# 1/|k| by Newton's method on GpSimd, in place of a square root on ScalarE, in a streaming encoder step

## The chip, the cores and the metric

The kernel runs on one core of a Trainium2 chip. The metric is the device time of one execution in microseconds (us); the figure for a kernel is the median of several runs. A core has five engines, each with a queue of its own that it works off in order: TensorE (PE; its weight loads are shown apart as PEld), VectorE (DVE), ScalarE (ACT), GpSimd (POOL) and SyncE (SP, which here issues the DMAs). The engines wait for each other by semaphores.

## The reference

One layer of an encoder on 1024 prompt frames and 32 frames of a running stream. One input projection feeds four branches; each is projected again, gated and summed; an output projection and a layer norm end it. The change lies in branch D, the gated delta rule, which works on eight heads of width 128:

```
def l2norm(x):
    return x * lax.rsqrt(jnp.sum(x * x, axis=-1, keepdims=True) + L2_EPS)
...
q = l2norm(qkv[..., :W_QK].reshape(bsz, l, H_D, DK))
k = l2norm(qkv[..., W_QK:2 * W_QK].reshape(bsz, l, H_D, DK))
beta = jax.nn.sigmoid(col(OFF_DB, H_D).astype(f32))
...
kb = k * beta[..., None]
a_mat = jnp.where(strict, jnp.einsum('nbhid,nbhjd->nbhij', kb, k) * decay, 0.0)
t_mat = a_mat + jnp.eye(c, dtype=a_mat.dtype)
u_base = lax.linalg.triangular_solve(t_mat, v * beta[..., None], left_side=True,
                                     lower=True, unit_diagonal=True)
```

So each frame of each head needs 1/|k|: one number per frame, from the sum of 128 squares.

## The kernel before

The 1056 frames lie along the free dimension, in chunks of 352 columns. A list of jobs runs on PE: each loads 128 columns of a weight matrix (512 KB, `wr`), splits it into a high part on ScalarE (`wh`, L179) and a low part on VectorE (`wl`, L181), and multiplies it with the normalised input, split likewise (`xh`, `xl`, L212), into PSUM tiles named `mm`, which ScalarE or VectorE evict. Weights are loaded one job ahead.

Beside the jobs run queues of background steps, written as Python generators. At fixed points of each job (`bg()`) every queue is advanced by its rate, so its instructions are recorded between the job's. The framework then orders the instructions of each engine and sets the semaphores; engines execute in that order. Two kinds of background step matter here:

- Convolutions (`conv`, L312, L315 and L318): ScalarE starts an accumulator, then VectorE adds one tap after another over about 1060 columns, 1.3 us each. There are short ones (4 taps, `acc`) and one of 31 taps per channel block (`accc`).
- `gdn_a(h)`, the first stage of the delta rule for head h, between about 100 and 460 us. Its PSUM tiles are named `aux`; there are four such banks, used in turn.

In `gdn_a` the frames of a head lie in nine groups of 128 (the ninth has the 32 frames of the running stream). For groups 0 to 3, 4 to 7 and 8 in turn, PE transposes k and q (L478), ScalarE squares each group with a sum along the row (L480, into `kss` and `qss`), and VectorE forms `ke` from the transposed k (L483), which frees the bank. Then come four numbers per frame, for all nine groups at once (tiles of 128x9): r2 = 1/(kss + eps), cb = beta r2, c2 = -cb e^g, and c1 = beta sqrt(r2), for which ScalarE takes the square root (L492). After that, for each set of groups: PE transposes v (L527) and VectorE multiplies it by c1 (R, L529), which frees the bank of the transposed v, and R is stored to memory (`d_r<-st`); PE multiplies k with k and q (L546, two groups of six matmuls); VectorE scales and masks the result (L537 with cb, L538 with EU), which frees those banks. The tiles `st` that hold R, A and PT have two buffers each in turn, so that L538 of a set waits for the store of R. ScalarE makes the decays by Abs and Exp (L505, L506, L508), GpSimd masks them (EU, L507), and VectorE scales q (L509). GpSimd also fills and copies the few history columns of each convolution (`pad`, L292 and L296; `st_d`, L304 and L305).

On ScalarE each of these functions needs a table: ACT_TABLE_LOAD stands ahead of an instruction whose function is not in the loaded one. Silu (L428), Sigmoid (L748), Exp and Sqrt alternate in this stretch.

## Time and profile before

| | |
|---|---|
| time, three runs | 2212.17, 2213.03 (median), 2217.18 us |
| profiled execution | 2218.46 us, of which the span from first to last instruction is 2216.8 |
| busy in the span | PE 2175.4, DVE 1652.8, ACT 998.4, POOL 187.3 us |
| granted TensorE clock, mean | 0.997 |
| ACT table loads, L492 | 8, of 1283 ns each |

The profiled execution is one run, by the hardware profiler. In rows of a timeline the columns are start and duration in us, engine, line, operation, out<-in with shapes, and count; a bracket tells how long the engine was idle ahead of it and what ended that. Rows of groups show count, busy us and mean ns, then the idle time ahead. Rows of waits read: who waited, for whom, us in total, times, longest. Rows of stretches give the length and the busy us of PE, PEld, DVE, ACT and POOL (instructions in brackets), the granted clock, and DMA figures.

### The profile page before, as it was taken

The page shows a single profiled execution, that of the slowest core. Times are in us where ns is not written, and L with a number is a line of the kernel's source. Part 1 is how long each engine was busy: PE and PEld are TensorE (multiplying, and loading weights), DVE is VectorE, ACT ScalarE, POOL GpSimd, SP SyncE. Part 2 cuts the span into 40 slices and gives each one's busy share as a digit, 9 for nine tenths or more (in the row PEclk, how much of TensorE's full clock was granted, in tenths as well). Part 3 has the DMA queues.
Part 4 walks back from the last instruction along what each step waited for, and adds up shares of the span by engine and source line. Part 5 has one row for each costly group of instructions (what it writes and reads, how often), then busy time and mean ns, then how long its engine had stood idle before and what let it go on. Part 6 is the DMA issues. An engine that isn't in the chain of part 4 may idle for free.

```text
span 2216.8 us, 38575 instructions
## 1 busy us (share of the span) xinstructions
PE 2175.4 (98%) x15334; PEld 2127.1 (96%) x15334; DVE 1652.8 (75%) x2668; ACT 998.4 (45%) x1938; POOL 187.3 (8%) x257
## 2 busy tenths in 40 slices
PE   7999999999999999999999999999999999999998
PEld 7998999999999998999999999999999999999986
DVE  8585898569994764788979879767767779745576
ACT  4587668621124543333444444467677345203200
POOL 2211332001010000000000000000000000000043
PEclk9999999999999999999999999999999999999999
DMA  6144445431227764224333323333333889975422
GB/s 238 49 129 111 120 125 140 116 122 58 69 58 231 228 185 115 83 89 134 100 117 114 122 97 131 111 106 130 128 117 124 324 329 330 333 244 174 137 88 85
DMA packets 198159, 323.70 MB, mean 146 GB/s; under 512 B 52793, under 2 KB 117131, under 8 KB 197659
## 3 DMA queue, kind: packets, MB, share of 16 engines
q1 hardware_dynamic: 197979, 321.25, 45.0%
q8 instruction: 120, 1.97, 0.4%
q14 instruction: 60, 0.49, 0.1%
HBM read 211.12 MB, written 110.06 MB: 145 GB/s over the span
## 4 chain that ended last, share of the span: by engine, by line
PE 78%; DVE 3%; ACT 2%; DMA 2%; issue 1%; SPq 0%; DVEq 0%; ACTq 0%
PE mm L212 34%; PE mm L1091 28%; PE mm L1455 4%; PE mm L224 3%; PE aux L1204 1%; PE mm L240 1%; DMA wr<-in_w_in 1%; PE mm L1435 1%; PE aux L719 1%; PE aux L699 1%; PE aux L706 1%; PE aux L718 1%; PE aux L690 1%; PE aux L655 0%; PE aux L649 0%
## 5 line engine op out<-in xcount | busy, mean ns | idle before, releaser
L315 DVE SCALAR_TENSOR_TENSOR accc<-padc,cols,accc 128x1086 f32<-128x1086 f32 (+1 forms) x249 | 335.6, 1348 | 8.9 <-ACT accc L312 7.1
L212 PE MATMUL mm<-xh,wh 128*128 128x352 f32 (+2 forms) x1600 | 292.8, 324 | 1.8 <-ACT xh L898 0.9
L212 PE MATMUL mm<-xl,wh 128*128 128x352 f32 (+2 forms) x1600 | 290.7, 323 | 0.0
L212 PE MATMUL mm<-xh,wl 128*128 128x352 f32 (+2 forms) x1568 | 286.2, 323 | 0.0
L212 PEld LDWEIGHTS mm<-xh,wh 128*128 128x128 f32 x1600 | 256.3, 189 | 3.6 <-DVE xh L896 1.1
L212 PEld LDWEIGHTS mm<-xl,wh 128*128 128x128 f32 x1600 | 256.3, 189 | 1.4 <-issue 0.4
L212 PEld LDWEIGHTS mm<-xh,wl 128*128 128x128 f32 x1568 | 251.1, 189 | 1.2 <-issue 0.2
L179 ACT CAST wh<-wr 128x1024 fp32r<-128x1024 f32 x96 | 100.6, 1048 | 299.8 <-PE mm L212 226.6
L1091 PE MATMUL mm<-xh,o 128*128 128x264 f32 x1152 | 216.8, 284 | 0.0
L1091 PEld LDWEIGHTS mm<-xh,o 128*128 128x128 f32 x1152 | 181.3, 188 | 0.0
L1091 PE MATMUL mm<-xl,o 128*128 128x264 f32 x576 | 163.8, 284 | 0.0
L1103 ACT COPY mu<-mm 128x264 f32<-128x264 f32 x216 | 80.2, 376 | 158.8 <-PE mm L1091 157.9
L181 DVE TENSOR_TENSOR wl<-wr,wh 128x1024 fp32r<-128x1024 f32 x96 | 117.0, 1218 | 32.1 <-ACT wh L179 20.8
L1091 PE MATMUL mm<-xh,wl 128*128 128x264 f32 x576 | 113.7, 287 | 3.8 <-ACT mu L1103 3.8
L1091 PE MATMUL mm<-th,o 128*128 128x264 f32 x576 | 113.1, 286 | 1.5 <-ACT mu L1103 1.4
L1091 PE MATMUL mm<-xh,wh 128*128 128x264 f32 x576 | 111.8, 285 | 1.1 <-ACT xh L1154 1.1
L1091 PE MATMUL mm<-th,wh 128*128 128x264 f32 x576 | 111.6, 285 | 0.0
L1091 PE MATMUL mm<-th,wl 128*128 128x264 f32 x576 | 111.0, 285 | 0.0
L1109 DVE TENSOR_TENSOR ev<-mm,mu 128x264 f32<-128x264 f32 x216 | 91.5, 427 | 25.1 <-ACT mu L1103 12.6
L1091 PEld LDWEIGHTS mm<-xl,o 128*128 128x128 f32 x576 | 108.3, 188 | 0.0
L1287 DVE TENSOR_TENSOR ev<-mm,ev 128x352 f32<-128x352 f32 x90 | 46.0, 522 | 82.6 <-PE mm L212 71.9
L1056 DVE TENSOR_TENSOR o<-wr,o 128x512 fp32r<-128x512 f32 x108 | 74.1, 686 | 40.9 <-ACT o L1055 40.4
(341 smaller groups left out, 4954.4 us busy)
## 6 DMA issues: line engine op xcount, KB each, us to landing
wr<-in_w_in SPq DMA_DIRECT2D x137, 512.0 KB, 3.7
d_z<-ev SPq DMA_DIRECT2D x64, 264.0 KB, 2.1
d_gate<-ev SPq DMA_DIRECT2D x64, 264.0 KB, 2.1
wr<-in_w_branch SPq DMA_DIRECT2D x32, 512.0 KB, 5.5
ev<-d_gate SPq DMA_DIRECT2D x30, 528.0 KB, 7.3
st<-d_t SPq DMA_DIRECT2D x28, 528.0 KB, 6.5
sl<-d_z SPq DMA_DIRECT2D x28, 528.0 KB, 7.2
d_mix<-ev SPq DMA_DIRECT2D x24, 528.0 KB, 3.6
```

Source lines behind the costliest of these rows:

```text
L179: act.copy(hi, raw)
L181: dve.tensor_sub(lo, raw, hi.bitcast(F32))
L212: pe.matmul(ps[:, :c[1]], lhsT=w[:, k, :], rhs=r(k)[:, cs(c)], start=(n == 0), stop=(n == len(todo) - 1))
L224: pe.matmul(ps[:, :c[1]], lhsT=w[:, k, :], rhs=r(k)[:, cs(c)], start=(n == 0), stop=(n == len(todo) - 1))
L240: pe.matmul(ps[:, :c[1]], lhsT=w[:, k, :], rhs=j.rhs[r](k)[:, cs(c)], start=(k == i == 0), stop=(k == KT - 1 and i == 2))
L315: dve.scalar_tensor_tensor(acc, pad[:, i:i + W], col(name, ci, i), acc, op0=OP.mult, op1=OP.add)
L1056: dve.tensor_sub(t[:, 4:8], src, t[:, 0:4].bitcast(F32))
L1091: pe.matmul(b, lhsT=w[:, wo + k, :], rhs=XS[name](p, k)[:, sl], start=(start and n == 0), stop=(stop and n == 11), skip_group_check=True)
L1103: act.copy(mu[name][:, c * HC:(c + 1) * HC], b)
L1109: dve.tensor_add(res[i][:, a:a + HC], b, mu[name][:, c * HC:(c + 1) * HC])
L1287: dve.tensor_mul(G[d][:, cs(c)], ps, G[d][:, cs(c)])
L1455: pe.matmul(ps, lhsT=a[k][:, ts], rhs=w[k][:, hs], start=(n == 0), stop=(n == len(todo) - 1))
```

## The change

The square root on ScalarE goes. VectorE makes a first value of 1/sqrt(kss + eps) out of the bits of the number, by a shift and a subtraction in integers read as such (two instructions). GpSimd scales kss + eps by -0.5 and then runs three Newton steps r1 <- r1 (1.5 - 0.5 (kss + eps) r1^2), four instructions each. VectorE multiplies the result with beta, as before. All tiles are 128x9.

```
         r2 = gp.tile([128, 9], F32, name="r2")
-        dve.tensor_scalar(r2, kss[:, :, h], L2_EPS, None, op0=OP.add)
-        dve.reciprocal(r2, r2)
+        k2 = gp.tile([128, 9], F32, name="k2")
+        r1 = gp.tile([128, 9], F32, name="r1")
+        dve.tensor_scalar(k2, kss[:, :, h], L2_EPS, None, op0=OP.add)
+        dve.reciprocal(r2, k2)
         dve.tensor_mul(cb[:, :, h], r2, beta[:, :, h])
         dve.scalar_tensor_tensor(c2[:, :, h], cb[:, :, h], -1.0, egc[:, :, h], op0=OP.mult, op1=OP.mult)
-        act.activation(r2, r2, AF.Sqrt)
-        dve.tensor_mul(c1[:, :, h], r2, beta[:, :, h])
+
+        I32 = mybir.dt.int32
+        dve.tensor_scalar(r1.bitcast(I32), k2.bitcast(I32), 1, None, op0=OP.logical_shift_right)
+        dve.tensor_scalar(r1.bitcast(I32), r1.bitcast(I32), -1.0, float(0x5f3759df), op0=OP.mult, op1=OP.add)
+        pool.tensor_scalar(k2, k2, -0.5, None, op0=OP.mult)
+        for _ in range(3):
+            pool.tensor_tensor(r2, r1, r1, op=OP.mult)
+            pool.tensor_tensor(r2, r2, k2, op=OP.mult)
+            pool.tensor_scalar(r2, r2, 1.5, None, op0=OP.add)
+            pool.tensor_tensor(r1, r1, r2, op=OP.mult)
+        dve.tensor_mul(c1[:, :, h], r1, beta[:, :, h])
```

Lines behind the change count 11 more in the changed kernel: c1 is L504 there (L493 before), R is L540 (L529), the matmul groups are L557 (L546). The framework orders the instructions anew. Three places, all in head 0, show what this does.

VectorE, before. L493 forms c1 (here `c_130`), L529 forms R from it, and L315 are taps of a convolution:

```order
L483 TENSOR_TENSOR st<-aux,eks 32x128
L488 TENSOR_SCALAR r_1490<-kss 128x9
L489 RECIPROCAL r_1490<-r_1490 128x9
L490 TENSOR_TENSOR cb<-r_1490,beta 128x9
L491 SCALAR_TENSOR_TENSOR c_131<-cb,egc 128x9
L315 SCALAR_TENSOR_TENSOR acc<-pad,cols,acc 128x1059 x2
L493 TENSOR_TENSOR c_130<-r_1490,beta 128x9
L529 TENSOR_TENSOR st<-aux,c_130 128x512
```

VectorE, now, at the same place:

```order
L490 TENSOR_SCALAR k_1491<-kss 128x9
L491 RECIPROCAL r_1490<-k_1491 128x9
L496 TENSOR_SCALAR r_1492<-k_1491 128x9
L492 TENSOR_TENSOR cb<-r_1490,beta 128x9
L497 TENSOR_SCALAR r_1492<-r_1492 128x9
L493 SCALAR_TENSOR_TENSOR c_131<-cb,egc 128x9
L315 SCALAR_TENSOR_TENSOR acc<-pad,cols,acc 128x1059
L504 TENSOR_TENSOR c_130<-r_1492,beta 128x9
L315 SCALAR_TENSOR_TENSOR acc<-pad,cols,acc 128x1059
L540 TENSOR_TENSOR st<-aux,c_130 128x512
```

Two instructions are added, and one of the two taps that stood ahead of c1 now stands between c1 and R. In heads 1, 2, 5 no tap stands between the first value (L497) and c1; in head 3 there are two, in head 4 two, in heads 6 and 7 small instructions. In heads 6 and 7 a weight split (L181) now stands between c1 and R.

GpSimd, now. The names `r_1492` and `r_1490` are r1 and r2, `k_1491` is k2:

```order
L305 COPY st_d<-pad 128x3
L498 TENSOR_SCALAR k_1491<-k_1491 128x9
L500 TENSOR_TENSOR r_1490<-r_1492 128x9
L501 TENSOR_TENSOR r_1490<-r_1490,k_1491 128x9
L502 TENSOR_SCALAR r_1490<-r_1490 128x9
L503 TENSOR_TENSOR r_1492<-r_1492,r_1490 128x9
```

The last four rows stand there three times, and the copies of the next convolution's history (L304, L305) follow them. Before, nothing stood between these copies and those ahead. Each of these instructions waits for a semaphore that tells of the one before. In head 3 a mask of the decays (L518, L507 before) of 128x512 stands right ahead of the chain.

ScalarE, before:

```order
L480 ACTIVATE junk,qss<-aux 32x128
L312 ACTIVATE acc<-pad,cols 128x1059
L492 ACT_TABLE_LOAD
L492 ACTIVATE r_1490<-r_1490 128x9
L418 COPY pad<-mm 128x352 x2
L179 CAST wh<-wr 128x1024
```

ScalarE, now:

```order
L480 ACTIVATE junk,qss<-aux 32x128
L312 ACTIVATE acc<-pad,cols 128x1059
L418 COPY pad<-mm 128x352 x2
L179 CAST wh<-wr 128x1024
L516 ACTIVATE E<-E 32x32
L519 ACT_TABLE_LOAD
```

The load and the root are gone, and the load for the exponential (L519, L508 before) stays. In the whole program 92 table loads are left of 102. On PE the same matmuls stand in nearly the same order: in head 0 the group L557 stands one matmul earlier, in head 2 the transposes of v and the groups behind them stand 18 matmuls of the jobs later, and elsewhere no group is moved by more than seven. After the stretch of `gdn_a` the order is the same but for a few instructions on each engine.

## The prediction

> **What bounds the kernel now.** I read the page first, then the stage table of the stretch in which the changed lines run (110 to 460 us, heads 0 to 7 of the delta branch), then who waits for whom there, and last the rows around each of the eight places, in order of time.

> ```profile
> PE 2175.4 (98%) x15334; PEld 2127.1 (96%) x15334; DVE 1652.8 (75%) x2668; ACT 998.4 (45%) x1938; POOL 187.3 (8%) x257
> PE 78%; DVE 3%; ACT 2%; DMA 2%; issue 1%; SPq 0%; DVEq 0%; ACTq 0%
> ...
> 110.00:460.00 350.00, 338.40 (x2205) 330.66 (x2204) 259.35 (x478) 251.31 (x574) 64.22 (x105) 1.00 0.47 124
> 460.00:900.00 440.00, 440.00 (x3040) 423.93 (x3039) 332.37 (x573) 145.20 (x332) 31.74 (x33) 1.00 0.44 131
> ```

> TensorE (PE) is busy for 98% of the span, and the chain that ended last is PE for 78%. So the time is PE's work, plus the holes in it. Then comes the stretch of the change (busy PE, weight load, VectorE, ScalarE, GpSimd): PE is busy 338.4 of 350 us, so it has 11.6 us of holes. A change here can win at most these, and it loses what it adds to them. What ends them, and what VectorE (DVE) waits for at the changed line:

> ```profile
> PE aux L478 <- DVE st L483: 6.1, 3, 4.4
> PE aux L478 <- ACT junk L480: 2.4, 3, 1.0
> PE aux L527 <- DVE st L483: 2.0, 2, 1.8
> PE aux L546 <- DVE st L538: 0.6, 1, 0.6
> PE aux L546 <- DVE st L529: 0.3, 1, 0.3
> ...
> DVE c L493 <- ACT r L492: 11.2, 5, 3.1
> ```

> The columns are total us, times, longest. PE waits for 11.4 us in all, all of it for VectorE or ScalarE (ACT) to free one of the four "aux" PSUM banks. VectorE waits at c1 (L493) in five of eight heads, 11.2 us in all, for the square root.

> **The change part by part.**

> *ScalarE.* It loses, in each head, the table load and the square root:

> ```profile
> 132.22 1.28 ACT L492 ACT_TABLE_LOAD   x1
> 133.52 0.21 ACT L492 ACTIVATE r<-r 128x9 f32<-128x9 f32 x1
> ```

> That is 8 x 1.49 = 11.9 us. The order has 92 table loads where it had 102, so two more go by themselves: 2.6 us. ScalarE thus gets 14.5 us back, of which only what PE waits for counts: at most the 2.4 us of "L478 <- ACT junk", which I book whole as a gain, and, one step removed, part of the 8.1 us for st L483, which itself waits for ScalarE's squares. I book none of that (rival C does). [...]

> *GpSimd.* It gains 13 steps per head on 128x9, each reading what the one before wrote. The trace has no such row. The nearest:

> ```profile
> L1443 POOL TENSOR_TENSOR padc<-padc,wh 128x1024 f32<-128x1024 f32 x8 | 20.0, 2505 | 0.6
> ...
> L899 POOL TENSOR_TENSOR xl<-z,xh 128x128 fp32r<-128x128 f32 x2 | 0.9, 456 | 0.5 <-ACT xh L898 0.5
> ...
> 312.54 0.19 POOL L304 COPY st_d<-pad 128x3 f32<-128x3 f32 x1 [2.75 <-ACT pad L418]
> ```

> From 128 to 1024 columns a product grows by (2505 - 456) / 896 = 2.29 ns a column, so at 9 columns it is 456 - 119 x 2.29 = 184 ns, as the copy of three columns (0.19). L1443 reads what the instruction before it wrote, and idles 0.6 / 8 = 0.075 us for that. So I take 0.26 us a step, an estimate: 3.1 us for the 12 steps behind the first value, 3.4 for all 13. Bounds: 0.19 (no wait between steps; 2.3 us) and 0.456 (the shortest product seen; 5.5 us). A gain below these is excluded, since all steps hang on each other.

> These steps share something with VectorE:

> ```profile
> 140.11 1.28 DVE L318 SCALAR_TENSOR_TENSOR ev<-pad,cols,acc 128x1024 f32<-128x1024 f32 x1 [1.00 <-PE aux L527]
> ...
> 227.84 0.20 POOL L507 TENSOR_SCALAR_AFFINE_SELECT EU<-E 32x32 f32<-32x32 f32 x1 [20.42 <-DVE Gb L509]
> 140.49 0.97 POOL L507 TENSOR_SCALAR_AFFINE_SELECT EU<-E 32x32 f32<-32x32 f32 x1 [1.99 <-ACT E L506]
> 258.53 6.05 POOL L507 TENSOR_SCALAR_AFFINE_SELECT EU<-E 128x512 f32<-128x512 f32 x1
> ```

> The same select takes 0.20 us alone, and 0.97 when it meets the convolution step L318: it ends at 141.46, just as L318 does (141.39). One takes 6.05 us while VectorE runs such steps back to back. I read this as GpSimd standing still while a long two-input instruction runs on VectorE. [...] It speaks against this change: a convolution step placed beside the chain covers none of it. Without that rule head 0, below, would lose 1.7 us instead of 3.0.

> *VectorE.* Two more small instructions per head (0.15 to 0.18 us each, about 0.35) stand ahead of c1. And c1 now waits for GpSimd: behind it in VectorE's queue stands R = transposed v times c1 (L529), whose end frees the aux bank for PE's next group (L546) and whose store must land before the product at L538. So the question in each head is how late R becomes, and how much of that lies in slack.

> *Head 0.* VectorE, then PE:

> ```profile
> 131.08 0.15 DVE L488 TENSOR_SCALAR r<-kss 128x9 f32<-128x9 f32 x1
> ...
> 132.24 2.68 DVE L315 SCALAR_TENSOR_TENSOR acc<-pad,cols,acc 128x1059 f32<-128x1059 f32 x2 [0.33 <-ACT acc L312]
> 134.84 0.18 DVE L493 TENSOR_TENSOR c<-r,beta 128x9 f32<-128x9 f32 x1
> 135.10 0.69 DVE L529 TENSOR_TENSOR st<-aux,c 128x512 f32<-128x512 f32 x1
> ...
> 135.86 0.38 PE L546 MATMUL aux<-kqh 128*128 128x256 f32 x1
> ```

> Today two convolution steps cover the root, and PE's group starts at 135.86, the moment R ends (135.79): no slack. In the new order one convolution step stands ahead of c1 and one behind it. The first value is there at about 132.0; one step fits before 132.24; then GpSimd stands until 133.56; the other 11 x 0.26 = 2.9 us end at 136.5. With c1 and the second convolution step R starts at 138.0, not 135.1. PE's group stands one matmul earlier, so it waits in full: **3.0 us**.

> *The other heads* (DVE at c1 and R, PE where it has a group soon after):

> ```profile
> 167.72 0.18 DVE L493 TENSOR_TENSOR c<-r,beta 128x9 f32<-128x9 f32 x1 [3.14 <-ACT r L492]
> 173.27 0.28 PE L546 MATMUL aux<-kqh 128*128 128x256 f32 x1
> ...
> 219.18 0.18 DVE L493 TENSOR_TENSOR c<-r,beta 128x9 f32<-128x9 f32 x1 [0.86 <-ACT r L492]
> 223.50 0.69 DVE L529 TENSOR_TENSOR st<-aux,c 128x512 f32<-128x512 f32 x1 [4.15 <-DMA d_ke<-st]
> ...
> 262.66 0.15 DVE L493 TENSOR_TENSOR c<-r,beta 128x9 f32<-128x9 f32 x1
> 269.31 0.76 DVE L538 TENSOR_TENSOR st<-aux,EU 128x256 f32<-128x256 f32 x2 [2.22 <-DMA d_r<-st]
> 270.75 0.28 PE L546 MATMUL aux<-kqh 128*128 128x256 f32 x1
> ...
> 311.04 0.17 DVE L493 TENSOR_TENSOR c<-r,beta 128x9 f32<-128x9 f32 x1
> 317.25 0.76 DVE L538 TENSOR_TENSOR st<-aux,EU 128x256 f32<-128x256 f32 x2 [0.60 <-DMA d_r<-st]
> 318.16 0.28 PE L546 MATMUL aux<-kqh 128*128 128x256 f32 x1
> ...
> 353.01 0.18 DVE L493 TENSOR_TENSOR c<-r,beta 128x9 f32<-128x9 f32 x1 [2.77 <-ACT r L492]
> 394.95 0.18 DVE L493 TENSOR_TENSOR c<-r,beta 128x9 f32<-128x9 f32 x1 [3.08 <-ACT r L492]
> 395.22 0.69 DVE L529 TENSOR_TENSOR st<-aux,c 128x512 f32<-128x512 f32 x1
> 395.98 0.28 PE L546 MATMUL aux<-kqh 128*128 128x256 f32 x1
> ...
> 434.85 0.18 DVE L493 TENSOR_TENSOR c<-r,beta 128x9 f32<-128x9 f32 x1 [1.31 <-ACT r L492]
> 438.49 0.69 DVE L529 TENSOR_TENSOR st<-aux,c 128x512 f32<-128x512 f32 x1 [1.47 <-PE aux L527]
> ```

> - Head 1: VectorE is free from 164.58 (167.72 less 3.14). Two convolution steps now go ahead of the chain (2.6), then 0.35 and 3.2 (chain and hops): c1 at 170.7, 3.0 late. R then ends at 171.7, and PE's group comes at 173.27: 0.
> - Head 2: 218.32 + 0.35 + 3.2 = 221.9, but R waits for a DMA until 223.50 anyway: 0.
> - Head 3: c1 is due at 263.0, but the chain stands behind the select that took 6.05 us, and all of it runs only once VectorE stops: 0.3, taken for the rest of the select, and 3.4 for the chain, so c1 at 266.7, 4.0 late. L538 waits for R's store, so it moves along; the first of its two ends at about 269.7, 1.0 ahead of PE's group at 270.75. PE loses 3.0 there. The last 1.0 I let it lose too, in a longer wait for st L483 (1.8 is the longest of the L527 row above): **4.0 us**.
> - Head 4: two convolution steps between the first value and c1 leave the chain standing: 311.04 + 0.35 + 3.2 = 314.6; one step of like length stands between c1 and R as before: 3.3 late after what small gaps give. L538's first ends at 317.67, PE's group comes at 318.16: **2.8 us**.
> - Head 5: 350.24 + 0.35 + 3.2 = 353.8, 0.8 late; no group of PE's near: 0.
> - Head 6: c1 as late as today, but a weight split (1.2 us) now stands ahead of R, which comes 1.0 later; PE's group follows R's end (395.91) by 0.07: **0.9 us**.
> - Head 7: 433.54 + 0.35 + 3.2 = 437.1, the split 1.2: 438.3, and R waits for PE until 438.49: 0.

> On SP's queue, R's stores and the weight loads behind them move by as much as R; the loads run a whole job ahead, so I book nothing. GpSimd's own state copies behind the chain wait 3 us longer, and no row shows anyone in a hurry for them. After 460 us the order hardly differs, and PE is busy for all 440 us from there to 900, so what is lost stays lost.

> **Sum:** 3.0 + 4.0 + 2.8 + 0.9 - 2.4 = +8.3 us. The profiled execution took 2218.46 us, so it would be 2226.8; it lies 5.4 above the median of the runs, 2213.03. On the median: 2213.0 + 8.3 = **2221.3 us**.

> **The rivals.**

> *B, covered.* Head 0 pays, but elsewhere VectorE catches up before PE notices: it is busy 259 of 350 us in this stretch. For it speak heads 1, 2, 5 and 7; against it the two places with 1.0 and 0.5 us of slack. +3.0 + 0.9 - 2.4 = +1.5: 2214.5.

> *C, faster.* ScalarE's 14.5 us bring its squares forward, and with them st L483 and PE's waits for both: 6.1 + 2.4 + 2.0 = 10.5 go, head 0 and 6 take 3.9: -6.6, 2206.4. It decides once more than 3.9 us of these waits go. For it: the longest, 4.4 us at L478, comes in a row of table loads. Against it: these are loads for the exponential and the sigmoid, most of which stay, and no square root stands near.

> *D, dearer steps.* At 0.456 us a step the chain is 5.5 us, 2.4 more; heads 0, 3, 4 and 6 pay it in full and heads 1, 5 and 7 some 0.5: +8.3 + 9.6 + 1.5 = 19.4, 2232.4. Spans on GpSimd are rough, which is for it; the copy of 0.19 is against it.

> That the change might not take away the table switches I rule out by the order.

> **How the numbers follow.** A, my sum: 0.50. B 0.28, C 0.14, D 0.08. About 0.2% (4.4 us) is what a measurement of this kernel can tell from no change. A and D lie above it, B within, C below: slower 0.58, same 0.28, faster 0.14. For the range I leave out most of C below and half of D above: steps of 0.19 us take 0.8 us off heads 0 and 6, which makes 2212.9 of B, and some of C's gain beside it 2210; up to 2231 for dearer steps. A's own range is 2217 to 2226.

> **What would show it.** Right: the thirteen steps at about 0.2 us with 0.07 between them; a row "DVE c <- POOL r" in place of "DVE c <- ACT r", with some 20 to 25 us over eight heads instead of 11.2; PE waits for st L540 and L549 (L529 and L538 today) of about 10 us where these have 0.9 now; PE busy as before. Wrong: PE's holes between 110 and 460 us stay at 11.6 us (B) or shrink (C); GpSimd steps of 0.4 us or more (D); no standstill of the steps beside convolution steps.

## The result and the profile after

The changed kernel took 2231.6 us in the median of 4 runs (2225.33 to 2235.55); the kernel before took 2214.49 beside it (4 runs). The ratio is 1.0066, with a 95% interval of 1.0052 to 1.0081: slower, by 14.6 us (11.5 to 17.9). I had forecast +8.3 and a range up to 2231. The median lies 0.6 above that end; the ratio, put on the 2213.03 from which I started, gives 2227.6, within it. Later, the runs of before had medians of 2215.5 to 2216.2 (15 to 23 runs each), so the three from which I started lay some 2.5 to 3 us low; ratios are the better measure here.

The profiled execution took 2229.87 us (span 2227.9), 11.4 more than the profiled one of before. Its page, the busy times and the chain that ended last:

```profile
PE 2181.5 (98%) x15334; PEld 2131.0 (96%) x15334; DVE 1654.6 (74%) x2684; ACT 983.6 (44%) x1920; POOL 211.4 (9%) x361
PE 75%; DVE 8%; ACT 4%; DMA 3%; issue 2%; POOL 1%; SPq 0%; DVEq 0%; ACTq 0%
```

ScalarE lost 14.8 us (forecast 14.5), GpSimd gained 24, and in the chain VectorE's share rose from 3% to 8%. The stage table, the row of the changed stretch (columns as before, then granted clock, DMA share and GB/s):

```profile
110.00:460.00 350.00, 330.83 (x2124) 321.77 (x2123) 256.30 (x483) 233.52 (x552) 83.86 (x208) 0.99 0.43 118
```

PE's holes went from 11.6 to 19.2 us, and the granted clock from 1.00 to 0.99. Who waits for whom there (total us, times, longest; L540 was L529, L549 was L538, L557 was L546, L538 was L527):

```profile
PE aux L557 <- DVE st L540: 7.6, 4, 2.6
PE aux L557 <- DVE st L549: 4.4, 2, 3.8
PE aux L478 <- DVE st L483: 2.5, 3, 0.9
PE aux L478 <- ACT junk L480: 2.2, 4, 0.8
PE aux L557 <- ACT junk L480: 1.4, 2, 1.1
PE aux L538 <- DVE st L483: 1.0, 2, 0.7
...
DVE c L504 <- POOL r L503: 26.1, 8, 3.6
```

VectorE now waits for GpSimd at c1 in all eight heads, and PE waits 12.0 us for st L540 and L549 where it waited 0.9. The other waits of PE fell from 10.5 to 7.1. Head 0 in the timeline (start, us, engine, line), the chain and its readers:

```profile
132.32 1.32 DVE L315 SCALAR_TENSOR_TENSOR acc<-pad,cols,acc 128x1059 f32<-128x1059 f32 x1 [0.34 <-ACT acc L312]
...
132.51 1.25 POOL L502 TENSOR_SCALAR r<-r 128x9 f32<-128x9 f32 x1
133.84 0.20 POOL L503 TENSOR_TENSOR r<-r,r 128x9 f32<-128x9 f32 x1
...
136.20 0.20 POOL L503 TENSOR_TENSOR r<-r,r 128x9 f32<-128x9 f32 x1
136.44 0.18 DVE L504 TENSOR_TENSOR c<-r,beta 128x9 f32<-128x9 f32 x1 [2.79 <-POOL r L503]
136.53 1.31 DVE L315 SCALAR_TENSOR_TENSOR acc<-pad,cols,acc 128x1059 f32<-128x1059 f32 x1
137.76 0.68 DVE L540 TENSOR_TENSOR st<-aux,c 128x512 f32<-128x512 f32 x1
...
138.50 0.58 PE L557 MATMUL aux<-kqh 128*128 128x256 f32 x1 [2.56 <-DVE st L540]
```

A GpSimd step that takes 0.24 elsewhere takes 1.25 and ends 0.12 after the convolution step on VectorE. From 133.84 to 136.20 there are eight steps, 0.295 us from start to start. c1 starts at 136.44 (I had 136.5), R at 137.76 (138.0), PE's hole is 2.56 (3.0). The other holes of PE for R and the product behind it:

```profile
180.09 0.36 PE L557 MATMUL aux<-kqh 128*128 128x256 f32 x1 [1.81 <-DVE st L540]
226.34 0.38 PE L557 MATMUL aux<-kqh 128*128 128x256 f32 x1 [1.76 <-DVE st L540]
274.53 0.35 PE L557 MATMUL aux<-kqh 128*128 128x256 f32 x1 [0.65 <-DVE st L549]
321.96 0.36 PE L557 MATMUL aux<-kqh 128*128 128x256 f32 x1 [1.49 <-DVE st L540]
328.16 0.35 PE L557 MATMUL aux<-kqh 128*128 128x256 f32 x1 [3.80 <-DVE st L549]
```

These are heads 1, 2, 3, 4 and 4.

```profile
134.77:138.18 3.41, 1.17 (x8) 0.88 (x6) 1.74 (x3) 1.05 (x1) 1.22 (x6) 1.00 0.00 0
138.18:141.60 3.42, 3.10 (x12) 3.10 (x13) 2.07 (x6) 0.52 (x2) 0.34 (x1) 0.50 0.36 100
141.60:145.01 3.41, 3.41 (x25) 3.40 (x24) 2.29 (x5) 2.76 (x6) 1.47 (x3) 1.00 0.51 128
175.73:179.14 3.41, 2.54 (x18) 2.23 (x16) 0.10 (x1) 0.45 (x1) 2.38 (x11) 1.00 0.23 65
179.14:182.56 3.42, 2.48 (x17) 2.51 (x18) 2.52 (x9) 0.49 (x3) 0.00 (x0) 1.00 0.29 89
182.56:185.97 3.41, 3.41 (x25) 3.41 (x24) 1.40 (x4) 2.32 (x3) 0.20 (x1) 1.00 0.48 127
223.52:226.93 3.41, 1.65 (x12) 1.36 (x11) 1.51 (x5) 1.04 (x1) 1.30 (x6) 1.00 0.26 73
226.93:230.34 3.41, 3.41 (x15) 3.41 (x14) 1.25 (x6) 0.49 (x3) 0.00 (x0) 0.50 0.53 147
```

After a window in which PE idled for 2.24 us (3.41 less 1.17) comes one at half clock, in which PE does 12 matmuls where the next does 25; likewise after 1.76 us of idle time (3.41 less 1.65). Head 1's hole of 1.81 us was cut by the grid into 0.87 and 0.94, and the clock stayed at 1.00. So the holes of heads 0 and 2 were paid twice: once themselves, and once more by up to 1.7 us (half of 3.41, an estimate). The changed kernel has four such stretches before its last microseconds (138, 227, 329 and 896 us), the kernel before has two (205, after the 4.45 us hole that ended at 204.78, and 1605).

The span grew by 11.1 us: PE's idle time by 5.0 (7.6 more in the stretch, 2.6 less elsewhere) and its busy time by 6.1. Two more half-clock stretches make some 3.4 of that, an estimate (2 x 1.7); 2.7 us I cannot assign. The four runs of the changed kernel had clocks of 0.998, 0.996, 0.995 and 0.993 with spans of 2223.4, 2227.9, 2231.4 and 2233.5, so the spread goes with the mean clock. One such stretch is 0.5 x 3.41 / 2228 = 0.0008 of it; from 0.998 to 0.993 that would be some six stretches more, an estimate, as only the second of the four runs has a trace.

### The profile page after: what moved, and what is told of

Same layout as the page of the kernel before. It is cut to its first block, busy times and chain, and to the rows that moved or that the text cites. A ratio compares the mean times of both kernels' runs of the same rounds, so it can differ in the third digit from the quotient of the medians.

```text
span 2227.9 us, 38678 instructions
## 1 busy us (share of the span) xinstructions
PE 2181.5 (98%) x15334; PEld 2131.0 (96%) x15334; DVE 1654.6 (74%) x2684; ACT 983.6 (44%) x1920; POOL 211.4 (9%) x361
## 4 chain that ended last, share of the span: by engine, by line
PE 75%; DVE 8%; ACT 4%; DMA 3%; issue 2%; POOL 1%; SPq 0%; DVEq 0%; ACTq 0%
PE mm L212 33%; PE mm L1102 26%; PE mm L1466 3%; PE mm L224 3%; DVE accc L315 2%; PE aux L1215 1%; PE mm L240 1%; DMA wr<-in_w_in 1%; PE mm L1446 1%; PE aux L730 1%; PE aux L710 1%; ACT junk L480 1%; PE aux L717 1%; PE aux L729 1%; PE aux L701 1%
## 5 line engine op out<-in xcount | busy, mean ns | idle before, releaser
L315 DVE SCALAR_TENSOR_TENSOR accc<-padc,cols,accc 128x1086 f32<-128x1086 f32 (+1 forms) x249 | 335.0, 1346 | 9.1 <-ACT accc L312 7.1
L181 DVE TENSOR_TENSOR wl<-wr,wh 128x1024 fp32r<-128x1024 f32 x96 | 117.1, 1220 | 29.5 <-ACT wh L179 18.8
```

The lines of the kernel that those rows point to most:

```text
L181: dve.tensor_sub(lo, raw, hi.bitcast(F32))
L315: dve.scalar_tensor_tensor(acc, pad[:, i:i + W], col(name, ci, i), acc, op0=OP.mult, op1=OP.add)
```

## Experiments

My theory after the result: VectorE stands at c1 (in order) until the chain on GpSimd ends; so R and the bank that it frees are late, PE gets holes, and half-clock stretches follow the long ones (2.24 and 1.76 us of idle time, above). Rival 1: the new order of instructions, or the two more on VectorE, cost the time, not the chain. Rival 2: GpSimd's steps cost by running beside VectorE, whoever waits. Rival 3: all of it is the work queued behind the waiting c1. Rival 4: the way to another engine and back.

| kernel | median us | ratio to before, 95% interval |
| --- | --- | --- |
| the change (three steps) | 2231.6 | 1.0066 [1.0052, 1.0081] |
| 1: first value only | 2215.36 | 0.9998 [0.9989, 1.0007] |
| 2: root used, chain unread | 2217.87 | 1.0010 [1.0001, 1.0019] |
| 3: six steps | 2246.12 | 1.0135 [1.0120, 1.0150] |
| 4: chain split in two | 2235.87 | 1.0091 [1.0077, 1.0104] |
| 5: one step | 2218.13 | 1.0010 [1.0001, 1.0018] |
| 6: c1 on GpSimd | 2229.38 | 1.0055 [1.0041, 1.0069] |
| 7: c1 on GpSimd, R late | 2212.42 | 0.9982 [0.9974, 0.9991] |
| 8: root, R late | 2207.40 | 0.9965 [0.9951, 0.9978] |
| 9: as 7, two steps | 2205.45 | 0.9958 [0.9946, 0.9971] |
| 10: two steps on VectorE, R late | 2204.28 | 0.9949 [0.9937, 0.9962] |
| 11: two steps on VectorE | 2217.22 | 1.0007 [0.9998, 1.0016] |

Runs 1 to 4, 5 to 8 and 9 to 11 each shared a chip and its runs of the kernel before. Edits are shown against the changed kernel, if nothing else is said.

**1. First value only.**

```
-        pool.tensor_scalar(k2, k2, -0.5, None, op0=OP.mult)
-        for _ in range(3):
...
         dve.tensor_mul(c1[:, :, h], r1, beta[:, :, h])
```

> The thirteen GpSimd steps are left out: c1 is made from VectorE's first value alone, good to some 3%, so the output differs. Theory (VectorE waits in order at c1 for the chain, R comes late, PE waits for R's bank): no wait for GpSimd is left, PE's holes between 110 and 460 us fall from 19.2 to 8 to 11 us, and the time is 2206 to 2215, 0.996 to 1.000 of before. Rival 1 (the new order, or the two extra VectorE steps, and not the chain): holes stay at 17 us or more and the time at 2224 or more. Half-clock stretches of 3.4 us: if PE's stalls bring them, one or two fewer than in after, mean clock 0.997 or more.

Measured: 2215.36, 0.9998. The stretch (stage table):

```profile
110.00:460.00 350.00, 339.50 (x2215) 331.03 (x2215) 260.71 (x495) 236.28 (x557) 53.25 (x105) 1.00 0.46 124
```

Holes of 10.5 us, as expected, and only one half-clock stretch before the end (881.91 us; mean clock 0.998, the change's 0.996). Rival 1 falls: with the extra VectorE steps kept and a new order (not quite that of the change, for the framework ordered anew), nothing is lost. The run also bears on what ScalarE's relief is worth: root and loads are gone here, and no chain takes their place, yet the time is that of before, within 0.1%. It shows the relief and the two VectorE steps together; what each is worth by itself is not shown.

**2. Root used, chain unread.**

```
-        dve.reciprocal(r2, k2)
...
+        r3 = gp.tile([128, 9], F32, name="r3")
+        dve.reciprocal(r3, k2)
...
-        dve.tensor_mul(c1[:, :, h], r1, beta[:, :, h])
+        act.activation(r3, r3, AF.Sqrt)
+        dve.tensor_mul(c1[:, :, h], r3, beta[:, :, h])
```

> The square root on ScalarE is back and makes c1; the first value and the thirteen GpSimd steps run beside it and nobody reads what they give. Theory: VectorE waits some 11 us for the root as in before, holes 10 to 13 us, time 2212 to 2219, 0.999 to 1.002 of before. Rival 2 (GpSimd's steps hold VectorE up in the memory, or fill its queue): holes 17 us or more, time 2224 to 2232.

Measured: 2217.87, 1.0010. GpSimd is busy for 35 us more in this stretch than in before, and VectorE waits for ScalarE alone:

```profile
110.00:460.00 350.00, 339.17 (x2204) 331.28 (x2204) 260.34 (x495) 250.10 (x574) 99.38 (x209) 1.00 0.46 124
```

```profile
DVE c L506 <- ACT r L505: 7.9, 4, 3.1
```

Rival 2 falls as the main cause: the same 13 steps, with nobody waiting, cost 2.2 us (0.2 to 4.2) of the 14.6.

**3. Six steps.** `for _ in range(6)` in place of `range(3)`.

> Six Newton steps in place of three: the chain is 25 steps, 3.5 us longer at 0.29 us a step. Theory: wait of VectorE for GpSimd at c1 from 26 to about 54 us, PE's holes between 110 and 460 us from 19 to 33 to 45 us, time 2246 to 2262, 1.014 to 1.022 of before; half-clock stretches more than in after, mean clock 0.993 or less. Rival 1 (order): 2226 to 2234.

Measured: 2246.12, 1.0135 (the expectation's low end was 1.014). The stage table and the waits:

```profile
110.00:460.00 350.00, 316.70 (x2016) 308.07 (x2017) 249.57 (x461) 230.39 (x544) 99.92 (x278) 0.97 0.41 114
```

```profile
PE aux L557 <- DVE st L540: 18.7, 4, 5.9
...
DVE c L504 <- POOL r L503: 43.7, 7, 7.1
```

PE's holes are 33.3 us and the clock in this stretch 0.97. The wait at c1 grew by 17.6 us, not 28: the order put a convolution step ahead of c1 in some heads. Three steps more cost 15.3 us (0.0069 x 2216), about as much as the first three. Rival 1, which gave 2226 to 2234, falls again.

**4. Chain split in two.** The new function holds k2, its reciprocal, the first value and the thirteen steps, on the columns s.

```
+        def newton(s):
+            dve.tensor_scalar(k2[:, s], kss[:, s, h], L2_EPS, None, op0=OP.add)
...
                 if src is kT:
+                    if c0 >= 4:
+                        newton(slice(0, 8) if c0 == 4 else slice(8, 9))
...
+        dve.tensor_mul(c1[:, 0:8, h], r1[:, 0:8], beta[:, 0:8, h])
...
+            if c0 == 8:
+                dve.tensor_mul(c1[:, 8:9, h], r1[:, 8:9], beta[:, 8:9, h])
             R = gt("st", 2)
```

> Same arithmetic, but the chain runs twice per head: for the first eight chunks as soon as their sums of squares stand, some 5 us earlier, and for the ninth chunk where it stood; c1 of the first eight is made where c1 stood, c1 of the ninth ahead of the R that reads it. Theory: the wait for GpSimd falls from 26 to 10 us or less where the order leaves the early chain ahead, holes 9 to 14 us, time 2208 to 2219. Rival 2 (GpSimd's steps beside VectorE cost, whoever waits): twice as many steps, so 2232 or more.

My expectation failed: 2235.87, 1.0091. VectorE's waits at the two products and, in head 0, the start of the early chain:

```profile
DVE c L509 <- POOL r L487: 24.6, 8, 3.6
DVE c L545 <- POOL r L487: 15.4, 7, 3.2
```

```profile
126.09 1.26 POOL L482 TENSOR_SCALAR k<-k 128x8 f32<-128x8 f32 x1 [3.45 <-DVE r L480]
127.39 1.21 POOL L484 TENSOR_TENSOR t<-r 128x8 f32<-128x8 f32 x1
```

The wait was not hidden but grew by half, from 26.1 to 40.0 us, and PE's holes came to 24.4 us (325.61 busy of 350). The framework set each c1 a few VectorE instructions behind its first value again, wherever the program had it, and the first two steps of the early chain took 1.26 and 1.21 us where the next three took 0.20 to 0.26; I read that as a standstill beside two convolution steps. So this is no run in which the chain is covered. Its time is what rival 2 said (2232 or more), and by itself it does not part the two; the rows of waits, and run 2, speak for the theory.

**5. One step.** `for _ in range(1)`.

> One Newton step in place of three: the chain is 5 GpSimd steps (some 1.5 us), 1/|k| is good to some 0.2%. Theory with the runs so far (no chain: +0; three steps: +14.6; six: +30): a stall of 1.5 us is mostly covered and brings no half-clock stretch, since PE's idle time in no window of 3.41 us passes 1.75 us; wait at c1 8 to 13 us, PE's holes between 110 and 460 us 10 to 14, time 2215 to 2221, 0.9995 to 1.002 of before. Rival (each step costs the same 5 us): 2221 and more.

Measured: 2218.13, 1.0010. The stretch and the wait:

```profile
110.00:460.00 350.00, 337.76 (x2205) 329.56 (x2204) 261.57 (x495) 236.10 (x556) 67.18 (x145) 1.00 0.45 124
```

```profile
DVE c L504 <- POOL r L503: 9.0, 8, 1.5
```

Holes of 12.2 us, as expected, and a granted clock of 1.00 where the change has 0.99. The cost is not in proportion to the steps: none costs -0.4 us, one 2.2, three 14.6, six 29.9. A wait of 1.1 us per head is mostly covered; the next 2 us are not.

**6. c1 on GpSimd.**

```
-        dve.tensor_mul(c1[:, :, h], r1, beta[:, :, h])
+        pool.tensor_tensor(c1[:, :, h], r1, beta[:, :, h], op=OP.mult)
```

> c1 itself is multiplied on GpSimd, so the chain is 14 steps and VectorE waits where R reads c1, not at c1; convolution steps and weight splits that stood behind c1 go ahead of the wait. Theory: where R stands right behind c1 (heads 1, 2, 5) nothing changes; in heads 0, 3, 4, 6, 7 VectorE does 1.2 to 1.3 us of work first, but the GpSimd chain stands still beside the convolution steps of heads 0, 3 and 4. Time 2224 to 2231, 1.003 to 1.007 of before, holes 15 to 19 us. Rival (the waiting place c1, with work queued behind it, is the whole cost): 2214 to 2220, holes 13 us or less.

Measured: 2229.38, 1.0055. VectorE's row is now the one of R:

```profile
DVE st L540 <- POOL c L504: 22.1, 6, 3.9
```

The holes stay at 18.9 us (331.08 busy of 350). Rival 3 falls: the waiting place hardly matters, since R itself stands next in the order.

**7 and 8. R late,** with c1 on GpSimd, and with the square root. The same seven lines, from the transposes of v to the yield behind R's store, are moved in both:

```
-            ps = aux()
...
-            R = gt("st", 2)
-            dve.tensor_mul(R[:L, :n], ps[:L, :n], bc(c1[:L, cr, h]))
...
             put("pt", PT[:L, :n, :L], c0, n, L, L)
             yield
+            ps = aux()
...
+            R = gt("Rt")
+            dve.tensor_mul(R[:L, :n], ps[:L, :n], bc(c1[:L, cr, h]))
...
```

> As the run with c1 on GpSimd, and R with its transposes of v is made behind each group's products of k and q instead of ahead of them (R in a tile of its own), so four to six evictions (1.4 to 2.2 us) and PE's products stand between the chain and its reader. Theory: the chain's 4 us are covered but for 1 to 2 us, PE waits for R's bank 4 us or less, holes 9 to 14 us, and the time is within 5 us of the same move with the square root (next run). Rival 2 (GpSimd's steps cost wherever they stand): 10 us or more above the next run.

> The kernel before (square root on ScalarE) with R moved behind the products in the same way: the control of the run above. Theory: R was seldom late there, so the move does little: 2210 to 2220, 0.998 to 1.002 of before, holes 9 to 14 us.

Measured: 2212.42 (0.9982) with the chain, 2207.40 (0.9965) with the root. Run 7, the stretch and the wait for GpSimd:

```profile
110.00:460.00 350.00, 342.36 (x2230) 334.68 (x2230) 260.65 (x488) 239.05 (x559) 96.80 (x218) 1.00 0.45 126
```

```profile
DVE Rt L570 <- POOL c L504: 4.9, 3, 2.5
```

The whole chain, one step longer than in the change, now costs 5.0 us over the root instead of 14.6: the products between it and its reader cover most of it, as the row of waits shows (4.9 us in three heads, where the change has 26.1 in eight).

For run 8 my expectation failed: it lies below the 2210 to 2220 that I gave it, so the move by itself gains some 8 us over before. The move does two things, since R also gets a tile of its own (`Rt`) in place of a share in the two `st` buffers, so that PT no longer waits for R's store. No run has one without the other, so what each is worth is not shown.

Holes are 7.6 us in run 7 and 7.0 in run 8 (343.01 busy), less than I expected of either, and only 0.6 apart. The mean clock of the profiled execution was 0.995 in run 7 and 0.999 in run 8, that of all of them 0.995 to 0.998 against 0.998 to 0.999. From 110 to 1600 us both have 1.00 in each row of the stage table; the last row, of run 7, then of run 8:

```profile
1600.00:2240.00 640.00, 599.56 (x3751) 578.75 (x3750) 410.26 (x559) 213.42 (x272) 55.38 (x40) 0.99 0.56 198
```

```profile
1600.00:2240.00 640.00, 593.56 (x3724) 572.88 (x3723) 409.11 (x557) 210.78 (x267) 55.71 (x40) 1.00 0.56 198
```

So most of the 5.0 seems to lie behind the stretch of the change. I did not test why.

**9. As 7, with two steps.** `for _ in range(2)`.

> R behind the products and c1 on GpSimd, with two Newton steps in place of three (1/|k| to some 5e-6): the chain is 10 steps, 2.9 us. Theory: what was left of the wait (4.9 us for R) goes, PE's holes between 110 and 460 us are 6 to 8 us, and the time comes to that of the moved R with the square root: 2205 to 2211, 0.996 to 0.998 of before. Rival 2 (GpSimd's steps cost wherever they stand): 2211 or more.

Measured: 2205.45, 0.9958, level with the root's 0.9965, as the intervals overlap. The wait for GpSimd:

```profile
DVE Rt L570 <- POOL c L504: 1.9, 2, 1.3
```

Holes are 6.3 us (343.67 busy). Ten GpSimd steps per head beside VectorE cost nothing to be seen once nobody waits for them.

**10. Two steps on VectorE, R late.** Run 7's move, and

```
+        for _ in range(2):
+            dve.tensor_tensor(r2, r1, r1, op=OP.mult)
+            dve.scalar_tensor_tensor(r2, r2, -0.5, k2, op0=OP.mult, op1=OP.mult)
+            dve.scalar_tensor_tensor(r1, r2, 1.5, r1, op0=OP.add, op1=OP.mult)
         dve.tensor_mul(c1[:, :, h], r1, beta[:, :, h])
```

> R behind the products, and two Newton steps on VectorE, each of three instructions, so that 1/|k| needs no other engine. Theory: six more small VectorE instructions per head (1.2 us) between products that PE waits for little: 2205 to 2212, 0.996 to 0.999 of before. If VectorE's time counts in this stretch: 8 x 1.2 = 10 us more than with the root, 2215 or more.

Measured: 2204.28, 0.9949, just below the range that I gave it. It has the lowest time here, 11.3 us (8.4 to 14.0) under before, though its interval does not part it from runs 8 and 9. The stretch:

```profile
110.00:460.00 350.00, 346.96 (x2272) 339.74 (x2271) 269.40 (x551) 238.59 (x559) 64.91 (x109) 1.00 0.47 132
```

Holes of 3.0 us. VectorE does 10 us more work than in before, and PE does not notice.

**11. Two steps on VectorE,** R where it was; the loop of run 10 alone.

> The same two Newton steps on VectorE with R where it was. Theory (what counts is when c1 is there, whatever engine makes it): in six heads c1 comes 1.3 us after the first value; in heads 3 and 4 the new order puts five or six convolution steps (6.5 to 8 us) between its steps, so R is some 5 us later there: 2215 to 2224, 1.000 to 1.004 of before. Rival 4 (the way to another engine and back is the cost): 2210 to 2216.

Measured: 2217.22, 1.0007, within the theory's range and 1.2 us above rival 4's; the interval does not part the two. Head 3 shows the mechanism, from its first to its last step:

```profile
260.06 0.15 DVE L499 TENSOR_TENSOR r<-r 128x9 f32<-128x9 f32 x1
...
266.87 0.16 DVE L502 TENSOR_TENSOR c<-r,beta 128x9 f32<-128x9 f32 x1
```

Six steps of 0.15 us took 6.8 us, since the order puts a convolution step of 1.3 us behind nearly each. Without another engine a late c1 is still a late c1; rival 4 stays open as a small part.

## Why the prediction was right, and where it was not

- **Direction and mechanism: right.** VectorE waits for GpSimd at c1 (26.1 us, forecast 20 to 25), PE for st L540 and L549 (12.0 us, forecast about 10). Runs 1, 2, 5 and 3 show the wait for the chain to be the cause.
- **The step: 0.26 us assumed, 0.295 measured** without a standstill (0.20 or 0.24 busy, 0.08 to the next). Near the assumed row and far from rival D's 0.456. The standstill of GpSimd beside convolution steps, on which 1.3 us of head 0 hung, is in the timeline: 1.25 us for a 0.24 us step, which ends at 133.76, 0.12 after the convolution step beside it (133.64).
- **Head by head** the forecast was 3.0, 0, 0, 4.0, 2.8, 0, 0.9, 0; measured 2.56, 1.81, 1.76, 0.65, 5.29 (1.49 + 3.80), and next to nothing in 5, 6 and 7. The sum, 10.7 against 12.1 by these rows, came out near by luck, as its terms did not. The step that failed: "PE where it has a group soon after" took PE's groups from the times of before. In head 1 I had R end at 171.7, ahead of a group at 173.27; in the new run the group was due at 178.28 (180.09 less 1.81) and R began at 179.25, because VectorE took up the last sums of squares 8.8 us later (172.52 against 163.76) and PE's groups came only 5.0 later. In head 2 I let R wait for a DMA until 223.50, which it did not do, and it came at 225.60. In head 3 PE's group came 3.1 us later than before and hid what I booked. In head 4 L549 waited 2.15 us for R's store (0.60 before), where I had it move along with R, and PE's group behind it waited 3.80.
- **ScalarE's relief: booked at -2.4, wrong.** PE's waits for ScalarE's squares rose from 2.4 to 3.6 us; those for st L483 fell from 8.1 to 3.5. But run 1, which has the relief, the two VectorE steps and no chain, is at 0.9998: nothing to be measured is left of the gain, and rival C falls with it. In the profiled run other holes moved, among them the 4.4 us one of before, so that the stretch's balance (+7.6) came near my +8.3, which is luck too.
- **Left out: the clock.** I turned holes into time one to one. In the traces of before and of the changed kernel a window at 0.50 followed each of the five windows with 1.76 us or more of idle time. That is the term that the sum put at nothing. In the profiled run idle time gave 5.0 of the 11.1 us and the clock some 3.4, an estimate; the runs with lower clocks took longer (0.998: 2223.4 us, 0.993: 2233.5). It is the likely reason why 14.6 was measured and not 8. How much of the 6.3 us between is the clock is not shown to the last us, since 2.7 us of PE's busy time stay unassigned.
- **Rival B** (covered) is what runs 5 and 9 show for a shorter chain or a later reader; in the change as it was, it fell.

## What to carry to other kernels

Here the off-loaded chain cost what its reader waited, not what its engine worked (35 us more of GpSimd with nobody waiting cost 2.2 us; 26.1 us of waiting at c1 went with 14.6 us): put its reader late enough in the program (here behind the products of k and q), or make the chain short, before you judge the engine it runs on. Moving the chain alone need not help: in run 4 the framework set the reader close behind it again. And look at TensorE's holes together with the granted clock: head 1's hole, cut into 0.87 and 0.94 us by two windows, cost only itself, while the five windows with 1.76 to 3.05 us of idle time were each followed by one at 0.50.

## What the runs showed of the hardware

In the traces of before and of the changed kernel (without the first 30 and the last 8 us), I summed PE's idle time in each window of the grid. Five windows have 1.76 us or more of it: 3.05 and 1.96 us in before (from 201.73 and 1601.20), 2.24, 1.76 and 2.24 us in the changed kernel (from 134.77, 223.52 and 325.92). After each comes a window at a clock of 0.50. Twenty windows have 0.82 to 1.55 us of it, and after each the clock stays at 1.00. In run 6 the clock is 0.50 after 1.90 us of idle time and 1.00 after 1.61:

```profile
178.92:182.33 3.41, 1.51 (x12) 1.25 (x10) 1.63 (x5) 0.45 (x1) 1.27 (x6) 1.00 0.03 10
182.33:185.74 3.41, 3.41 (x14) 3.41 (x13) 1.27 (x5) 0.49 (x3) 0.20 (x1) 0.50 0.54 147
349.59:353.00 3.41, 1.80 (x12) 1.53 (x11) 3.41 (x5) 3.41 (x14) 1.32 (x2) 1.00 0.17 46
353.00:356.41 3.41, 3.11 (x21) 2.81 (x20) 3.41 (x4) 3.28 (x16) 1.57 (x1) 1.00 0.80 262
```

The 1.75 us that I named ahead of run 5 was my estimate: these rows have 1.55 and 1.61 us with a clock of 1.00 behind, and 1.76 with one of 0.50. Run 1 has a shorter hole in the head in which the change has its 1.76 us (223.52 above):

```profile
223.14:226.55 3.41, 2.05 (x15) 1.84 (x14) 2.38 (x6) 0.82 (x1) 0.20 (x1) 1.00 0.48 126
226.55:229.97 3.42, 3.42 (x23) 3.36 (x22) 3.42 (x9) 3.40 (x4) 0.23 (x2) 1.00 0.63 117
```

Here 1.36 us of idle time, and a clock of 1.00 after it.

One stretch at 0.50 has no idle time ahead of it. In the changed kernel, at 895.94, it follows a window in which PE is busy for all 3.41 us and all matmuls are on small tiles of 32 rows or 32 columns. But another window of such tiles alone, three windows earlier, is followed by full clock (the first two rows are that window and the one behind it):

```profile
882.29:885.71 3.42, 3.42 (x25) 1.79 (x23) 0.94 (x4) 0.91 (x3) 0.00 (x0) 1.00 0.24 77
885.71:889.12 3.41, 3.41 (x24) 3.17 (x24) 3.12 (x10) 2.62 (x9) 1.31 (x2) 1.00 0.00 0
...
892.53:895.94 3.41, 3.41 (x25) 1.90 (x24) 3.41 (x10) 0.37 (x1) 0.44 (x2) 1.00 0.20 49
895.94:899.36 3.42, 3.42 (x13) 3.04 (x13) 1.89 (x5) 2.39 (x10) 0.73 (x1) 0.50 0.67 240
```

Run 1 has one behind a window in which PE is busy throughout:

```profile
878.50:881.91 3.41, 3.41 (x23) 1.70 (x22) 3.41 (x8) 0.14 (x2) 0.93 (x2) 1.00 0.20 42
881.91:885.32 3.41, 3.41 (x13) 3.41 (x13) 2.09 (x6) 2.27 (x10) 0.24 (x1) 0.50 0.60 220
```

In before the same matmuls run from 879.47 to 883.5, and no stretch at 0.50 follows until 1604.61. So the small tiles alone do not explain it, and what brings it stays open.
